# The source and the piece size of ten accumulating DMAs in a weight-streaming decoder layer

## The chip, the cores and the metric

The kernel runs on one core of a Trainium2 chip. The metric is the device time of one execution in microseconds; lower is better. The time of a version is the median of its runs.

## The reference, cut to what matters

One layer of a decoder trunk is computed for 256 tokens of width 2048, all in float32: a gated conformer branch and a block-sparse attention branch, cross attention to 256 memory tokens, and a SwiGLU feed-forward part. The change touches only the feed-forward part, whose first product takes most of its weights' bytes:

```
def swiglu(h, w_in, w_out):
    g, u = jnp.split(h @ w_in, 2, axis=-1)
    return (jax.nn.silu(g) * u) @ w_out
...
        h = rmsnorm(x, norm_ffn_g[l])
        x = x + swiglu(h, w_ffn_in[l], w_ffn_out[l])
```

`w_ffn_in` has 2048 rows and 2 x 5632 columns.

## The kernel before, in words

**Split products.** Each float32 matrix product is made of three passes of TensorE. Both factors are split into a high part (the value rounded to float32r, a narrower format that TensorE takes at full rate) and a low part (the value minus its high part). `mm3` (lines 426 to 431) then issues high x high (L429), high x low of the weights (L430) and low x high (L431). L430 is thus the first line that reads the weights' low part.

**Blocks, pairs, units.** The weights are streamed from DRAM once. A block covers 1024 columns of a weight matrix, two halves of 512, for all rows. The feed-forward part's first product is made of the blocks ffn0 to ffn10, each with 512 columns of the gate half and 512 of the other half, so that a row's two pieces lie far apart in DRAM. A block walks over 8 pairs of 128 rows (1 MB of weights each, 4 pieces of 512 columns on 128 partitions). A pair is either one plain unit (kind W, 8 products of `mm3`) or two units of a scheme of Strassen's kind with 7 products (kinds a and b), for which VectorE first forms sums of the four pieces.

**Places.** A pair's weights land in a raw place (`raw`, 1 MB); during the feed-forward blocks there are five. They are loaded by SP in the order of the pairs, four DMAs of 256 KB a pair (`load_unit`, lines 719 to 736), each as soon as the place is free; SP's queue works in order, so that a load that waits holds all loads behind it. The high and the low part of a unit stand in a place for weights, one of five in this part, called `whi`/`wlo` or `w` in the profile. TensorE's last product with it makes it free.

**The usual way.** ScalarE casts `raw` to the high part (`cast_one`), VectorE subtracts it from `raw` and writes the low part (`step_one`, L832, shown as L97 in the profile, the line of a wrapper round all such calls). Then the raw place is free.

**The way of ten units.** `ADDED_LOW` (line 39) names pair 0 of each of ffn1 to ffn10. For these, `subtract_on_way` (lines 738 to 744) lets ScalarE write the negated high part into the low part's place. Then GpSimd issues DMAs that add the raw weights to it as they are written (`accum_op`). VectorE has no part in it. Before the change, these DMAs read the weights a second time from DRAM: two DMAs, one for each half of 512 columns, each of 128 partitions x 2 rows x 2 KB. The raw place is free after ScalarE's cast.

**What sets the order.** The order of all engines' instructions is written out when the program is built, by a planner that keeps an estimated clock of TensorE, VectorE, ScalarE and the loads (`self.clock`). `ADDED = 8.0` (line 40) is its estimate of the microseconds from ScalarE's end to the low part's landing; `leave_raw` (lines 844 to 848) tells it when a raw place is free. The semaphore waits follow from which instruction reads and writes which place. Beside these ten units GpSimd moves other things by DMA: in the feed-forward part it writes the block's results to DRAM (L1997, `md`) and reads them back later (L2026).

## Time and profile before

| | |
|---|---|
| median of 3 runs | 1709.81 us (1707.27 to 1713.94) |
| the profiled execution's own time | 1708.28 us |
| its span, first to last instruction | 1706.5 us |
| granted TensorE clock | 0.997 |
| ScalarE (ACT) busy | 1035.5 us, 61% of the span |
| read from DRAM | 351.97 MB |

The engines are PE (TensorE's products), PEld (its weight loads), DVE (VectorE), ACT (ScalarE), POOL (GpSimd) and SP (SyncE, which issues loads). A name with q stands for the engine's sequencer. Tiles are named out<-in without buffer numbers, so `w<-in_w_ffn_in` is a transfer from the weights in DRAM to a place for weights. Rows of waits give who waited for what, the sum in us, how often and the longest. Rows of the timeline give the start and the duration in us, the instruction, and in brackets the idle time just before it and what ended it; x8 there stands for several of one form in a row. Rows of the chain give start, duration and what the chain ran through.

### The profile page before, as it was taken

The numbers are of one execution on the slowest core, as the hardware profiler recorded it, in microseconds if no ns is written. First come the engines' busy times: TensorE is split into PE (matmuls) and PEld (weight loads), VectorE is DVE, ScalarE is ACT, GpSimd is POOL, SyncE is SP. The second block draws the span as 40 slices with busy tenths as digits, with TensorE's granted clock in tenths as the row PEclk, the third lists the DMA queues.
The fourth block names the chain that finished last, engine by engine and source line by source line (L and its number), as shares of the span: only waits on it lengthen the run. The fifth ranks groups of instructions, "written<-read, shape, count | busy, mean of one in ns | idle before, by whom it ended". The sixth has DMA issues, their size and how long they took to land. (4 is left out here: it accounts for less than half of the span.)

```text
span 1706.5 us, 20882 instructions
## 1 busy us (share of the span) xinstructions
PE 1668.4 (98%) x7586; PEld 1377.8 (81%) x7586; DVE 1448.9 (85%) x1470; ACT 1035.5 (61%) x1142; POOL 88.7 (5%) x147
## 2 busy tenths in 40 slices
PE   9999999999999999999999999999999999999998
PEld 7888888888888888888888877787777777888886
DVE  7889989898778898977888989878878877999797
ACT  7565768887545686655556665555555545665563
POOL 0000000000000010000001000000000001110100
PEclk9999999999999999999999999999999999999999
DMA  8656555566666776645556778677667767787773
GB/s 290 215 205 219 192 186 179 172 217 205 196 209 208 228 241 209 210 148 186 174 173 203 277 221 252 197 211 239 208 208 230 211 205 234 241 295 246 263 236 124
DMA packets 147479, 365.42 MB, mean 214 GB/s; under 512 B 17040, under 2 KB 17296, under 8 KB 147376
## 3 DMA queue, kind: packets, MB, share of 16 engines
q1 hardware_dynamic: 131904, 322.36, 57.5%
q0 software_dynamic: 14608, 40.54, 8.3%
q8 instruction: 59, 0.97, 0.2%
q10 hardware_dynamic: 864, 1.19, 0.2%
q14 instruction: 44, 0.36, 0.1%
HBM read 351.97 MB, written 12.06 MB: 213 GB/s over the span
## 5 line engine op out<-in xcount | busy, mean ns | idle before, releaser
L97 DVE TENSOR_TENSOR wlo<-raw,whi 128x1024 fp32r<-128x1024 f32 (+3 forms) x234 | 397.5, 1707 | 77.8 <-ACT whi L97 75.6
L97 ACT CAST whi<-raw 128x1024 fp32r<-128x1024 f32 (+3 forms) x237 | 341.6, 1448 | 135.2 <-PE bank L431 109.0
L430 PE MATMUL bank<-wlo,op 128*128 128x512 f32 x911 | 356.6, 391 | 8.7 <-DMA wlo<-in_w_ffn_in 8.7
L429 PE MATMUL bank<-whi,op 128*128 128x512 f32 x911 | 358.9, 394 | 0.0
L431 PE MATMUL bank<-whi,op 128*128 128x512 f32 x911 | 356.1, 391 | 0.0
L430 PE MATMUL bank<-w,op 128*128 128x512 f32 x750 | 293.7, 392 | 17.8 <-DMA w<-in_w_ffn_in 17.6
L429 PE MATMUL bank<-w,op 128*128 128x512 f32 x750 | 294.7, 393 | 0.0
L431 PE MATMUL bank<-w,op 128*128 128x512 f32 x750 | 292.2, 390 | 0.0
L97 DVE TENSOR_TENSOR w<-raw,w 128x1536 fp32r<-128x1536 f32 (+2 forms) x100 | 203.8, 2041 | 20.7 <-ACT w L97 19.8
L97 ACT CAST w<-raw 128x2048 fp32r<-128x2048 f32 (+2 forms) x107 | 184.1, 1727 | 45.1 <-PE bank L431 26.4
L430 PEld LDWEIGHTS bank<-wlo,op 128*128 128x128 f32 x911 | 171.8, 189 | 46.1 <-DMA wlo<-in_w_ffn_in 11.5
L431 PEld LDWEIGHTS bank<-whi,op 128*128 128x128 f32 x911 | 171.6, 188 | 36.1
L429 PEld LDWEIGHTS bank<-whi,op 128*128 128x128 f32 x911 | 171.8, 189 | 34.4
L430 PEld LDWEIGHTS bank<-w,op 128*128 128x128 f32 x750 | 140.8, 188 | 51.2 <-DMA w<-in_w_ffn_in 22.3
L429 PE MATMUL bank<-whi,xh 128*128 128x512 f32 x449 | 178.4, 397 | 0.2 <-ACT whi L97 0.2
L430 PE MATMUL bank<-wlo,xh 128*128 128x512 f32 x449 | 175.3, 390 | 0.3
L431 PE MATMUL bank<-whi,xl 128*128 128x512 f32 x449 | 175.1, 390 | 0.0
L431 PEld LDWEIGHTS bank<-w,op 128*128 128x128 f32 x750 | 140.8, 188 | 29.2
L429 PEld LDWEIGHTS bank<-w,op 128*128 128x128 f32 x750 | 140.8, 188 | 28.1
L97 ACT CAST w<-sums 128x2048 fp32r<-128x2048 f32 x42 | 80.4, 1914 | 84.1 <-DVE sums L97 59.7
L97 DVE TENSOR_TENSOR w<-sums,w 128x2048 fp32r<-128x2048 f32 x42 | 96.1, 2289 | 25.1 <-ACT w L97 24.9
L97 DVE TENSOR_TENSOR c<-bank,c 128x512 f32<-128x512 f32 x153 | 102.5, 686 | 5.3 <-PE bank L431 0.4
(218 smaller groups left out, 2111.8 us busy)
## 6 DMA issues: line engine op xcount, KB each, us to landing
raw<-in_w_ffn_in SPq DMA_DIRECT2D x352, 256.0 KB, 4.3
raw<-in_w_in SPq DMA_DIRECT2D x84, 512.0 KB, 4.2
raw<-in_w_ffn_out SPq DMA_DIRECT2D x62, 512.0 KB, 5.1
raw<-in_w_ckv SPq DMA_DIRECT2D x48, 512.0 KB, 4.5
raw<-in_w_in SPq DMA_DIRECT2D x72, 256.0 KB, 4.5
raw<-in_w_ffn_out SPq DMA_DIRECT2D x52, 256.0 KB, 4.7
raw<-in_w_out SPq DMA_DIRECT2D x24, 512.0 KB, 5.1
raw<-in_w_cq SPq DMA_DIRECT2D x24, 512.0 KB, 5.1
```

The source lines that it names most:

```text
L97: return f(out, *args, **kwargs)
L429: mm(out, lhs[0], rhs[0], start=start, stop=False)
L430: mm(out, lhs[0], rhs[1], start=False, stop=False)
L431: mm(out, lhs[1], rhs[0], start=False, stop=stop)
```

## The change

The accumulating DMAs of the ten units read the raw weights from their raw place in SBUF and no longer from DRAM. The two DMAs become one, over the whole 128 x 2048 tile, so that each partition's piece is one run of 8 KB in source and destination. The raw place is now read by this DMA, so that SP's next load into it waits for its landing too; the planner is told that it is free `ADDED` later.

```
-    def subtract_on_way(self, x, hi, lo):
+    def subtract_on_way(self, src, hi, lo):
 
         self.act.activation(lo, hi.bitcast(F32), AF.Copy, scale=-1.0)
-        rows = slice(2 * x.p * P, (2 * x.p + 2) * P)
-        for j, (w, c) in enumerate(x.blk.cols):
-            self.nc.gpsimd.dma_start(
-                lo[:, j::2, :], w[rows, c : c + 512].rearrange("(i p) n -> p i n", p=P), accum_op=ALU.add)
+        lo, src = (y.rearrange("p a n -> p (a n)") for y in (lo, src))
+        self.nc.gpsimd.dma_start(lo, src, accum_op=ALU.add)
...
         if x.added:
-            self.subtract_on_way(x, *self.w[v])
-            self.leave_raw(x, t["act"])
+            self.subtract_on_way(src, *self.w[v])
+            self.leave_raw(x, t["act"] + ADDED)
```

In the built program the order of the instructions of every engine is the same before and after, apart from the ten DMAs that stand in place of twenty on GpSimd. Ten loads of SP, one in each of ffn1 to ffn10, wait for one more semaphore.

## The prediction

> **What bounds the kernel now.** I read the page's shares first, then the waits of TensorE, then the chain of work round one of those waits.

> ```profile
> PE 1668.4 (98%) x7586; PEld 1377.8 (81%) x7586; DVE 1448.9 (85%) x1470; ACT 1035.5 (61%) x1142; POOL 88.7 (5%) x147
> PE 28%; DMA 7%; ACT 1%; issue 1%; DVE 1%; POOL 0%; DVEq 0%; ACTq 0%
> ```

> TensorE is busy for 98% of 1706.5 us, so it idles for 1706.5 - 1668.4 = 38.1 us in all, and an edit can only win from that idle time (and from the restarts after it). The second row is the chain that ended last: 7% of it is DMA, far more than ScalarE or VectorE. The list of TensorE's waits says which DMA:

> ```profile
> PE bank L430 <- DMA w<-in_w_ffn_in: 17.6, 13, 2.3
> PE bank L430 <- DMA wlo<-in_w_ffn_in: 8.7, 6, 2.3
> ```

> Only the accumulating DMAs of L743 write `w` or `wlo` from `in_w_ffn_in` (plain loads write `raw`). So 17.6 + 8.7 = 26.3 us of the 38.1 us, in 13 + 6 = 19 waits, are TensorE standing at line 430, the first product that reads a low part, until such a DMA lands. There are ten such units, the first pair of each of the blocks ffn1 to ffn10, two DMAs each; 19 of the 20 are late, by 26.3 / 10 = 2.63 us a block. The chain through ffn3 shows how:

> ```profile
> 1088.20 0.24 PE bank L431
> ...
> 1088.51 1.93 ACT w L97
> ...
> 1090.46 1.93 ACT w L97
> ...
> 1092.68 0.43 POOL w L743
> ...
> 1093.38 13.84 DMA w<-in_w_ffn_in
> ...
> 1107.27 0.50 PE bank L430
> ```

> TensorE frees a place for weights at 1088.4, ScalarE casts the high part and writes the negated copy (2 x 1.93 us), GpSimd issues at 1092.68, and the second DMA (issued at 1093.38) lands 13.84 us later. The start of this chain hangs on TensorE's own earlier work, so the room from GpSimd's issue to TensorE's need stays as it is when everything shifts.

> **What a wait costs beyond its idle time.** Four products in a row, the third after a stop without recorded idle time:

> ```profile
> 1005.66 0.39 PE L431 MATMUL bank<-w,op 128*128 128x512 f32 x1
> 1005.89 0.39 PE L429 MATMUL bank<-w,op 128*128 128x512 f32 x1
> 1006.29 0.50 PE L430 MATMUL bank<-w,op 128*128 128x512 f32 x1
> 1006.62 0.40 PE L431 MATMUL bank<-w,op 128*128 128x512 f32 x1
> ```

> Starts are 0.23 us apart while TensorE runs; here they are 0.40 and 0.33. So a stop loses (0.40 - 0.23) + (0.33 - 0.23) = 0.27 us on top of recorded idle time (a product's recorded time overlaps the next one's). For 19 waits: 5.1 us. If all the waits go, the gain is 26.3 + 5.1 = **31.4 us**.

> **When the low part is needed.** Issue and need, in three blocks (ffn3, ffn8, ffn9; ffn3's issue stands above):

> ```profile
> 1103.38 0.50 PE L430 MATMUL bank<-w,op 128*128 128x512 f32 x1 [1.81 <-DMA w<-in_w_ffn_in]
> 1107.27 0.50 PE L430 MATMUL bank<-w,op 128*128 128x512 f32 x1 [1.79 <-DMA w<-in_w_ffn_in]
> ```
> ```profile
> 1321.07 2.45 POOL L743 DMA_DIRECT2D wlo<-in_w_ffn_in  x2 [22.75 <-DVE sums L97]
> 1366.26 2.39 POOL L743 DMA_DIRECT2D w<-in_w_ffn_in  x2 [42.74 <-DVE sums L97]
> ```
> ```profile
> 1330.64 0.50 PE L430 MATMUL bank<-wlo,op 128*128 128x512 f32 x1 [0.67 <-DMA wlo<-in_w_ffn_in]
> 1376.25 0.50 PE L430 MATMUL bank<-w,op 128*128 128x512 f32 x1 [1.89 <-DMA w<-in_w_ffn_in]
> ```

> The first need is the start less the idle time: 1101.57, 1329.97 and 1374.36, which is 8.89, 8.90 and 8.10 us after the issue. Before, the first columns' DMA meets that need and the second columns' DMA may come 2 products later. After, one DMA serves both, so all of its 1 MB has to land within about 8.1 to 8.9 us; before, the second landing came at 13.8 us in ffn3 (the answer for line 743 in that window):

> ```profile
> DMA to landing us min/median/max: 10.7/12.3/13.8
> ```

> **When the new DMA lands.** No trace here shows an accumulating DMA from SBUF or one with 8 KB pieces, so I bound it. Rows of the DMA view for 1000 to 1426 us, and of the landing times of line 1997 (256 KB, SBUF to DRAM, plain):

> ```profile
> q1 hardware_dynamic: 43285, 78.83, 57.5%
> q0 software_dynamic: 6800, 14.94, 16.2%
> ...
> md<-mid POOLq DMA_DIRECT2D x18, 256.0 KB, 4.1
> ```
> ```profile
> DMA to landing us min/median/max: 2.3/4.0/6.5
> ```

> The window holds 426 x 16 = 6816 us of DMA engines. Plain loads: 57.5% = 3919 us for 78.83 MB, 49.7 us a MB. GpSimd's queue: 16.2% = 1104 us; less 18 x 0.262 = 4.72 MB of `md` at 49.7 (235 us) leaves 869 us for 10.2 MB of accumulation, 85 us a MB. So 1.05 MB of accumulation costs 1.05 x 85 / 16 = 5.6 us of all engines, and at the plain price it would cost 3.3 us. Fixed part: the fastest `md` takes 2.3 us, of which 0.26 x 49.7 / 16 = 0.8 is data, so 1.5 us. That gives 1.5 + 3.3 = 4.8 us as the low end. The high end is the old pair's 13.8 us. I take 1.5 + 5.6 = **7.1 us**, the accumulating rows' own price per byte, since nothing shows that a longer piece or the other source changes it.

> The old 13.8 us is long because the engines were full of loads at the same time (share and GB/s at the end of the row):

> ```profile
> 1101.50:1107.50 6.00, 2.40 (x12) 1.75 (x12) 6.00 (x8) 1.89 (x3) 0.59 (x1) 1.00 0.99 265
> ```

> The edit removes that rivalry by a side effect: the raw place is no longer free at the cast but when the accumulating DMA has landed, and SP's queue is in order. SP's next load into that place waits, and all loads behind it stand too:

> ```profile
> 1090.45 0.33 SPq L735 DMA_DIRECT2D raw<-in_w_ffn_in  x1
> ...
> 1092.30 5.60 SPq L731 DMA_DIRECT2D raw<-in_w_ffn_in  x8
> 1109.57 0.33 SPq L735 DMA_DIRECT2D raw<-in_w_ffn_in  x1
> ```

> In ffn3 the load at 1090.45 is the one that waits; these 4 + 8 loads, 3 MB, mostly ran beside the accumulation before and come behind it after. So the DMA runs nearly alone there: 7.1 us against 8.9 of room, no wait. In ffn1, ffn2, ffn5 and ffn8 one whole load (4 issues, 1 MB, 3.3 us of all engines) goes out just ahead of the one that waits, as here in ffn8:

> ```profile
> 1319.13 0.33 SPq L735 DMA_DIRECT2D raw<-in_w_ffn_in  x1
> ```

> It is about half done when the accumulation starts, so I add 1.5 us: 8.6 us against 8.9. Too close to call; I allow 0.35 us of wait and a restart in three of these blocks (ffn1 had no first wait, so it has more room): 3 x 0.62 = 1.9 us.

> [...]

> **What the held loads cost.** In ffn3 SP's load slips from 1090.45 to 1092.68 + 7.1 = 1099.8, 9.3 us. The 3 MB then need 3 x 3.3 = 9.9 us, so the first MB is there at about 1099.8 + 5 = 1105 and the last at about 1111. ScalarE first reads the first of them here:

> ```profile
> 1114.01 3.53 ACT L97 CAST w<-raw 128x2048 fp32r<-128x2048 f32 x2
> ```

> If this is 3.6 us earlier after, 1110.4, some 5 us remain. ffn1 has the least room:

> ```profile
> 1002.12 0.38 SPq L735 DMA_DIRECT2D raw<-in_w_ffn_in  x1
> ```
> ```profile
> 1023.11 1.91 ACT L97 CAST w<-raw 128x2048 fp32r<-128x2048 f32 x1
> ```

> Issue at 1001.34 + 8.6 = 1010 and 5 us to land make 1015 against 1023. I cost the hold at nothing; its cover is the loads' lead over the casts, and without the cover each late us would count once a block, 10 us in all.

> **What is late next.** VectorE and ScalarE could keep TensorE's old pace. But what they idle for after a block's start is TensorE itself:

> ```profile
> 1245.09 0.59 ACT L97 COPY mid<-bank 128x512 f32<-128x512 f32 x1 [6.74 <-PE bank L443]
> ```
> ```profile
> 1246.33 0.75 DVE L97 SCALAR_TENSOR_TENSOR raw<-c,ss,raw 128x512 f32<-128x512 f32 x1 [3.53 <-ACT raw L97]
> ```

> ScalarE waited 6.74 us for transposes that stand behind the late products, VectorE 3.53 us behind ScalarE. Both move with TensorE, so no new wait. GpSimd issues one DMA in place of two (10 fewer), and nothing on it was late. DRAM reads fall by 10.5 MB, of no worth by itself. The engines' instructions and their order are otherwise the same.

> **The sum.** 31.4 - 1.9 = 29.5 us. The profiled execution took 1708.28 us, so 1678.8; it lies 1.5 us under the median of the three runs (1709.81), so the median after is 1680.3, say **1680**.

> **The rivals.** (a) The accumulation is dearer or is cut into the old 2 KB pieces (the change would then not do what it says): with 4 x 128 pieces the issue would take about as long as now, 2.4 us in place of some 0.6, so 7.1 + 1.8 = 8.9, or 10 us beside loads. At 9.9 us each block waits 1.2 + 0.27, 14.7 us in all: 1709.8 - 31.4 + 14.7 = **1693**. For it: nothing shows 8 KB pieces. Against it: even so it beats 13.8. (b) Slower: one landing for both halves. TensorE's first products no longer go ahead with half of the low part; if the DMA lands at x us, a block loses x - 8.7 + 0.27 where it lost 2.63 + 0.51 = 3.14, so it decides from x = 11.6. At twice the price, 1.5 + 11.2 = 12.7 us, it loses 4.3: 10 x 1.13 = 11 us slower, **1721**; at the old 13.8, 22 us slower, 1732. For it: both operands and the result now lie in SBUF, in the same partitions. Against it: the engines are emptied of loads. (c) The held loads come late to the casts by 2 to 3 us a block and eat the gain: 1680 + 25 = **1705**. Against it: the 5 and 8 us left above.

> **Chances and range.** Forecast (1674 to 1686) 0.70; (a) 1686 to 1700, 0.13; (c) and other near-draws 0.07; (b) 0.10. The range runs from 1674 (all waits gone, and 4 us as the runs before scatter) to 1697, which leaves out (b), (c) and a part of (a), some 0.2. Faster by over 0.5% (8.5 us, about what a measurement of this kernel can tell from no change): 0.83; within 0.5%: 0.07; slower: 0.10.

> **What would show it.** In the profile after: ten accumulating DMAs of 1 MB that land 7 to 9 us after their issue; TensorE's waits for them under 3 us in total where 26.3 stood; SP's wait for these DMAs, about 7 to 9 us in each block; a DMA share that falls to the accumulation alone while it runs; no new wait of ScalarE for `raw`. Landings over 11.6 us, or casts that wait for `raw`, would prove me wrong.

## The result, and the profile after

The changed kernel took **1681.36 us** (median of 4 runs, 1679.54 to 1682.95) against 1710.66 us for the kernel before (4 runs, 1707.27 to 1713.94): a ratio of 0.9829 (95% interval 0.9806 to 0.9851). Its profiled execution took 1681.37 us with a span of 1679.6 us, 26.9 us under the span before. The accumulating DMA is L742 there, the load issues keep L731 to L736, and the lines behind the change stand two lower.

The page's shares and its chain of the kernel after:

```profile
PE 1663.9 (99%) x7586; PEld 1378.5 (82%) x7586; DVE 1448.1 (86%) x1470; ACT 1033.4 (62%) x1142; POOL 72.6 (4%) x137
...
PE 89%; DMA 5%; DVE 3%; issue 1%; ACT 1%; SPq 0%; DVEq 0%; ACTq 0%; POOLq 0%
```

TensorE now idles for 1679.6 - 1663.9 = 15.7 us where it idled for 38.1; that is 22.4 of the 26.9 us. The other 4.5 us are less busy time for the same 7586 products. TensorE's waits after (sum, times, longest):

```profile
PE bank L430 <- DVE wlo L97: 1.5, 1, 1.5
PE bank L430 <- DMA wlo<-raw: 1.3, 1, 1.3
PE bank L430 <- DMA w<-raw: 1.0, 1, 1.0
```

The 19 waits on the accumulating DMAs (26.3 us) have become two (2.3 us), and there is one new wait of 1.5 us on VectorE. The answer for the accumulating line, and the DMA share while one of its ten DMAs runs (ffn3's, us, PE, PEld, DVE, ACT, POOL, granted clock, DMA share, GB/s):

```profile
L742 POOL DMA_DIRECT2D w<-raw x7: 863/886/891, 1003.5 to 1388.1; - x7
L742 POOL DMA_DIRECT2D wlo<-raw x3: 874/886/891, 1050.4 to 1303.3; - x3
...
DMA to landing us min/median/max: 7.0/7.8/9.3
```
```profile
1093.50:1098.70 5.20, 5.20 (x25) 4.30 (x24) 2.26 (x3) 3.75 (x3) 0.00 (x0) 1.00 0.93 187
```

Ten DMAs land 7.0 to 9.3 us after their issue, where the second of a pair landed up to 13.9 us after its own issue. While ffn3's runs, nothing else does: 187 GB/s over 5.2 us is 0.97 MB, nearly the DMA's own 1.05 MB, against 265 GB/s of mixed traffic before. SP shows why. Its queue stands until the landing (the waits of SP on these DMAs, and the issues of ffn3, which stood at 1090.45 before):

```profile
SPq L735 <- DMA w<-raw: 79.3, 7, 13.0
...
SPq L731 <- DMA wlo<-raw: 27.2, 3, 9.2
```
```profile
1099.00 0.33 SPq L735 DMA_DIRECT2D raw<-in_w_ffn_in  x1
...
1100.85 4.23 SPq L731 DMA_DIRECT2D raw<-in_w_ffn_in  x8
```

The change moves three things at once: the source (DRAM or SBUF), the number and piece size of the DMAs (two of 2 KB or one of 8 KB), and the hold of SP's loads until the landing. The theory to test was the prediction's: the **hold** wins, because the DMA then runs alone. The rivals: the **source**, and the **pieces**.

### The profile page after: what moved, and what is told of

It is laid out like the page before. It is cut to its first block, busy times and chain, and to the rows that moved or that the text cites. A ratio compares the mean times of both kernels' runs of the same rounds, so it can differ in the third digit from the quotient of the medians.

```text
span 1679.6 us, 20886 instructions
## 1 busy us (share of the span) xinstructions
PE 1663.9 (99%) x7586; PEld 1378.5 (82%) x7586; DVE 1448.1 (86%) x1470; ACT 1033.4 (62%) x1142; POOL 72.6 (4%) x137
## 4 chain that ended last, share of the span: by engine, by line
PE 89%; DMA 5%; DVE 3%; issue 1%; ACT 1%; SPq 0%; DVEq 0%; ACTq 0%; POOLq 0%
PE bank L430 29%; PE bank L431 29%; PE bank L429 29%; PE bank L443 2%; DMA raw<-in_w_ffn_in 2%; DMA wlo<-raw 2%; DMA w<-raw 1%; DVE w L97 1%; DVE sums L97 1%; DVE wlo L97 1%; ACT w L97 0%; DVE c L97 0%; ACT whi L97 0%; DMA vecs<-in_vecs 0%; PE bank L1547 0%
## 5 line engine op out<-in xcount | busy, mean ns | idle before, releaser
L97 DVE TENSOR_TENSOR wlo<-raw,whi 128x1024 fp32r<-128x1024 f32 (+3 forms) x234 | 397.6, 1707 | 76.7 <-ACT whi L97 74.9
L97 ACT CAST whi<-raw 128x1024 fp32r<-128x1024 f32 (+3 forms) x237 | 341.3, 1447 | 131.0 <-PE bank L431 106.5
L430 PE MATMUL bank<-wlo,op 128*128 128x512 f32 x911 | 355.3, 390 | 3.0 <-DVE wlo L97 1.5
L429 PE MATMUL bank<-whi,op 128*128 128x512 f32 x911 | 357.8, 393 | 0.0
L431 PE MATMUL bank<-whi,op 128*128 128x512 f32 x911 | 354.9, 390 | 0.0
L429 PE MATMUL bank<-w,op 128*128 128x512 f32 x750 | 294.6, 393 | 0.0
L430 PE MATMUL bank<-w,op 128*128 128x512 f32 x750 | 292.3, 390 | 1.2 <-DMA w<-raw 1.0
L431 PE MATMUL bank<-w,op 128*128 128x512 f32 x750 | 292.2, 390 | 0.0
L97 DVE TENSOR_TENSOR w<-raw,w 128x1536 fp32r<-128x1536 f32 (+2 forms) x100 | 203.9, 2041 | 17.8 <-ACT w L97 17.8
L97 ACT CAST w<-raw 128x2048 fp32r<-128x2048 f32 (+2 forms) x107 | 183.9, 1726 | 45.2 <-PE bank L431 28.8
L430 PEld LDWEIGHTS bank<-wlo,op 128*128 128x128 f32 x911 | 171.2, 188 | 39.0 <-DMA wlo<-raw 2.7
L431 PEld LDWEIGHTS bank<-whi,op 128*128 128x128 f32 x911 | 171.0, 188 | 35.9
L429 PEld LDWEIGHTS bank<-whi,op 128*128 128x128 f32 x911 | 171.1, 188 | 34.3
L429 PE MATMUL bank<-whi,xh 128*128 128x512 f32 x449 | 179.5, 400 | 0.2 <-ACT whi L97 0.2
L430 PE MATMUL bank<-wlo,xh 128*128 128x512 f32 x449 | 176.2, 392 | 0.1
L431 PE MATMUL bank<-whi,xl 128*128 128x512 f32 x449 | 176.0, 392 | 0.0
L430 PEld LDWEIGHTS bank<-w,op 128*128 128x128 f32 x750 | 140.9, 188 | 30.4 <-DMA w<-raw 1.3
L431 PEld LDWEIGHTS bank<-w,op 128*128 128x128 f32 x750 | 140.8, 188 | 29.5
L429 PEld LDWEIGHTS bank<-w,op 128*128 128x128 f32 x750 | 140.9, 188 | 28.1
L97 ACT CAST w<-sums 128x2048 fp32r<-128x2048 f32 x42 | 80.4, 1914 | 92.2 <-DVE sums L97 81.5
L97 DVE TENSOR_TENSOR w<-sums,w 128x2048 fp32r<-128x2048 f32 x42 | 96.2, 2290 | 17.2 <-ACT w L97 17.1
L97 DVE TENSOR_TENSOR c<-bank,c 128x512 f32<-128x512 f32 x153 | 102.6, 687 | 5.3 <-PE bank L431 0.4
## 6 DMA issues: line engine op xcount, KB each, us to landing
raw<-in_w_ffn_in SPq DMA_DIRECT2D x352, 256.0 KB, 4.6
raw<-in_w_in SPq DMA_DIRECT2D x72, 256.0 KB, 4.6
raw<-in_w_ffn_out SPq DMA_DIRECT2D x52, 256.0 KB, 4.5
```

Of the source, the lines that this page charges most:

```text
L97: return f(out, *args, **kwargs)
L429: mm(out, lhs[0], rhs[0], start=start, stop=False)
L430: mm(out, lhs[0], rhs[1], start=False, stop=False)
L431: mm(out, lhs[1], rhs[0], start=False, stop=stop)
```

## The experiments

Medians, with the ratio to the runs of the kernel before on the same chip:

| kernel | source | DMAs | loads held | us (range) | ratio (95%) |
|---|---|---|---|---|---|
| after | SBUF | 1, 8 KB | yes | 1681.36 (1679.54 to 1682.95) | 0.9829 (0.9806 to 0.9851) |
| two_sbuf | SBUF | 2, 2 KB | yes | 1674.69 (1674.54 to 1675.35) | 0.9795 (0.9781 to 0.9810) |
| two_sbuf_swapped | SBUF | 2, 2 KB, late one first needed | yes | 1680.27 (1678.72 to 1681.30) | 0.9820 (0.9804 to 0.9836) |
| dram_hold | DRAM, a rest from SBUF | 2, 2 KB, and a small one | yes | 1676.61 (1674.45 to 1677.29) | 0.9803 (0.9787 to 0.9820) |
| longer_hold | SBUF | 1, 8 KB | longer | 1683.28 (1682.08 to 1686.75) | 0.9845 (0.9825 to 0.9865) |
| no_hold | SBUF | 1, 8 KB | no | 1716.64 (1715.59 to 1721.05) | 1.0044 (1.0027 to 1.0060) |
| two_no_hold | SBUF | 2, 2 KB | no | 1713.98 (1710.64 to 1718.34) | 1.0016 (1.0004 to 1.0028) |
| swapped_dram | DRAM | 2, 2 KB, late one first needed | no | 1741.78 (1738.59 to 1746.40) | 1.0189 (1.0168 to 1.0210) |
| swapped_warm | the same | the same, with extra products | no | 1727.50 (1726.38 to 1731.82) | 1.0101 (1.0082 to 1.0121) |

**two_sbuf: the new source and the hold, with the two DMAs of before.** Against the kernel after:

```
-        lo, src = (y.rearrange("p a n -> p (a n)") for y in (lo, src))
-        self.nc.gpsimd.dma_start(lo, src, accum_op=ALU.add)
+        for j in range(2):
+            self.nc.gpsimd.dma_start(lo[:, j::2, :], src[:, j::2, :], accum_op=ALU.add)
```

> Two DMAs of 512 KB from the raw place in SBUF, one for each half of the columns, with 2 KB pieces: the source and the hold of the changed kernel, the number and the piece size of the kernel before. Theory H (the held loads leave the DMA engines to the accumulation, and that is what makes it land early; source and piece size count little): the first DMA lands 5 to 6 us after its issue, the second 7.5 to 9 us after the first issue, TensorE waits under 4 us in total for them, time 1678 to 1685 us. Rival P (the long pieces or the single DMA make it fast): the second lands 10 to 13 us after the issue as before the change, waits of 10 to 25 us, 1693 to 1706 us.

1674.69 us, below the expected range and faster than the kernel after (every run of the one lies below every run of the other, though the intervals of the two ratios overlap). TensorE's only wait on the DMAs, and the landings of its twenty DMAs:

```profile
PE bank L430 <- DMA wlo<-raw: 0.8, 1, 0.8
```
```profile
DMA to landing us min/median/max: 5.1/7.4/9.6
```

The first halves land as early as 5.1 us after their issue. One landing for both halves therefore costs something: the change's own step to one DMA takes back 4 to 6 us of what the rest gains. (Between the two profiled executions it is 6.0 us, but 2.0 of them are a slow start of the kernel after that the edit does not touch; it is shown below.)

**two_sbuf_swapped: the same pair in the other order**, so that the first products need the later DMA, as they need the only DMA of the kernel after. Against two_sbuf:

```
-        for j in range(2):
+        for j in (1, 0):
```

> The two DMAs from SBUF with 2 KB pieces and the hold, issued in the other order, so that TensorE's first products need the one that lands last (it landed 7.6 to 10.4 us after the first issue in the run with the right order). Theory E (two DMAs beat one because the half that is needed first lands at 5 to 6 us): it gives that back and is no better than the single DMA: 1679 to 1685 us, waits of 2 to 6 us in total in the blocks where loads run beside. Rival: the 2 KB pieces themselves, or what runs beside them, are better: 1673 to 1677 us as with the right order.

1680.27 us, 5.6 us back (4.3 us by the ratios, as the two ran on different chips) and 1.1 us from the kernel after. TensorE's waits:

```profile
PE bank L430 <- DMA w<-raw: 2.3, 4, 1.4
PE bank L430 <- DMA wlo<-raw: 2.0, 3, 1.5
```

The waits and their restarts, 3.5 + 6 x 0.27 = 5.1 us, make up the 5.2 us between the two spans (1678.8 and 1673.6). So it is the early landing of the first half that two_sbuf has over the kernel after, and the piece size leaves no difference in the time that I could tell from these runs' scatter.

**dram_hold: the old source, with the hold.** The two DMAs read DRAM as before; the last 64 columns of the second half are added by a small third DMA from the raw place, which holds SP's loads:

```
+        for j, (w, c) in enumerate(x.blk.cols):
+            n = 512 - 64 * j
+            self.nc.gpsimd.dma_start(
+                lo[:, j::2, 0:n], w[rows, c : c + n].rearrange("(i p) n -> p i n", p=P), accum_op=ALU.add)
+        self.nc.gpsimd.dma_start(lo[:, 1::2, n:], src[:, 1::2, n:], accum_op=ALU.add)
```

> Two DMAs from DRAM with 2 KB pieces as before, but the last 64 columns of the second half come from the raw place by a third, small DMA, so that the raw place is held until about the landing and SP's loads wait (all but one 256 KB load in most blocks). Theory H: the accumulation runs nearly alone though its source is DRAM: second landing 8 to 9.5 us after the first issue, the small one within 1 us more, waits of 2 to 10 us in total, time 1681 to 1692 us. Rival P (SBUF source or long pieces needed): landings of 10 to 13 us, 1698 to 1712 us.

1676.61 us, below the expected range. TensorE's waits on the DMAs, and SP's:

```profile
PE bank L430 <- DMA wlo<-raw: 1.4, 2, 1.0
```
```profile
SPq L736 <- DMA w<-raw: 72.6, 7, 10.6
...
SPq L731 <- DMA wlo<-raw: 29.9, 3, 10.2
```

More than the whole gain of the change is there, 33.9 us, with 15 of 16 weights still read from DRAM. The source is not the cause.

**no_hold: the new source and the one DMA, without the hold.** The DMA adds another tile of SBUF of the same shape (a left factor), so that the raw place is free at the cast as before; the ten units' low parts are other numbers:

```
-        lo, src = (y.rearrange("p a n -> p (a n)") for y in (lo, src))
-        self.nc.gpsimd.dma_start(lo, src, accum_op=ALU.add)
+        lo = lo.rearrange("p a n -> p (a n)")
+        self.nc.gpsimd.dma_start(lo, self.lefts["x3"]["quad"][0].bitcast(F32), accum_op=ALU.add)
...
-            self.leave_raw(x, t["act"] + ADDED)
+            self.leave_raw(x, t["act"])
```

> One DMA with 8 KB pieces from SBUF as in the changed kernel, but it adds another tile (a constant left factor of the feed-forward part) and not the raw weights, so the low parts hold other numbers, and SP's loads are not held. Theory H: 1.1 to 1.5 MB of loads run beside it, the first packet comes late, it lands 9.5 to 11.5 us after the issue, TensorE waits 1 to 2.5 us in each block, time 1692 to 1706 us. Rival P (the long pieces take the engines by themselves): it lands within 9 us, time 1679 to 1686 us.

1716.64 us, 0.4% slower than before and dearer than I expected. TensorE's waits, and the landings:

```profile
PE bank L430 <- DMA w<-op: 19.4, 6, 4.3
PE bank L430 <- DMA wlo<-op: 8.6, 3, 3.5
```
```profile
DMA to landing us min/median/max: 10.0/11.9/12.6
```

Without the hold the one DMA lands at a median of 11.9 us in place of 7.8, and TensorE waits 28.0 us in 9 long waits where the kernel before had 26.3 us in 19. The whole gain, and a little more, is gone with the hold. The waits alone are 1.7 us longer than before; most of the 12.8 us between the two spans (1719.3 and 1706.5) goes with the granted clock, 0.989 against 0.997, and 0.008 x 1719 is 14 us.

**two_no_hold: the new source with the two DMAs of before, without the hold.** The same stand-in tile in no_hold's loop of two:

```
+        src = self.lefts["x3"]["quad"][0].bitcast(F32).rearrange("p (a n) -> p a n", a=4)
+        for j in range(2):
+            self.nc.gpsimd.dma_start(lo[:, j::2, :], src[:, j::2, :], accum_op=ALU.add)
```

> Two DMAs from SBUF with 2 KB pieces that add a constant left factor and not the raw weights (the low parts hold other numbers), so that SP's loads are not held: against the kernel before only the source differs. Theory H: the source counts little, the loads beside it set the landing: first 9 to 10.7 us, second 11.5 to 14 us, waits of 22 to 30 us, 1704 to 1714 us. Rival S (reading SBUF and not DRAM speeds the accumulation): second landing under 10.5 us, 1680 to 1695 us.

1713.98 us (10 runs). Waits and landings are those of before (26.3 us in 19; 9.0/11.1/13.9):

```profile
PE bank L430 <- DMA w<-op: 15.4, 12, 2.3
PE bank L430 <- DMA wlo<-op: 11.1, 6, 2.3
```
```profile
DMA to landing us min/median/max: 9.3/11.1/13.8
```

This kernel differs from the one before in the source alone (with other numbers in it), and its DMAs land no sooner for it.

**longer_hold: the hold made longer.** Behind each accumulating DMA of the kernel after, a plain DMA copies the raw place to a scratch place in DRAM, which keeps it occupied some microseconds more:

```
+        self.nc.gpsimd.dma_start(self.marks["scratch"], src)
```

> The changed kernel, and behind each accumulating DMA a plain DMA of the same 1 MB from the raw place to a scratch tensor in DRAM, which nothing reads: the loads are held some 3 to 4 us longer and the engines move 10.5 MB more. Theory H says the loads' lead over the casts covers a hold of 7 to 9 us with 1 to 9 us to spare (the least in ffn7 and ffn4), so a longer hold begins to show there: ScalarE waits for loads of up to 3 us in two to four blocks, TensorE behind it for less, 1681 to 1690 us. Rival (the lead is far larger than needed): no change, 1679 to 1683 us. Rival (the loads were already the limit): 10 x 3 us more, 1705 us or over.

1683.28 us, 2 us over the kernel after. SP's waits on these DMAs:

```profile
SPq L735 <- DMA scratch<-raw: 63.4, 7, 15.3
SPq L731 <- DMA scratch<-raw: 35.9, 3, 12.4
...
SPq L735 <- DMA w<-raw: 35.1, 3, 12.0
```

SP stood for 134.4 us in place of 106.5, and it cost about 2 us, which is within the scatter of the two kernels. ScalarE waits long for weights of the feed-forward's first product only once, 7.4 us in ffn1, and for a load that goes out ahead of the hold. The loads' lead over the casts covers the hold with room left.

**swapped_dram: what a later first landing costs.** The kernel before with its two DMAs issued in the other order, so that the first products need the later one:

```
-        for j, (w, c) in enumerate(x.blk.cols):
+        for j, (w, c) in reversed(list(enumerate(x.blk.cols))):
```

> The kernel before, with its two DMAs from DRAM issued in the other order, so that TensorE's first products need the DMA that lands last: the same as one landing for both halves, at the landing time of before. By the break-even of the prediction (a block loses x - 8.9 + 0.27 us where it lost 3.14, with second landings of 12.3 to 14.6 us, 13.3 on average) it is 10 x 1.5 = 15 us slower than before: 1720 to 1732 us, ten waits of 3.5 to 6 us each. Rival: which half comes first does not matter, because TensorE meets the second landing in either case: 1707 to 1714 us.

1741.78 us, more than I expected. TensorE's waits, its busy time, and two stretches round ffn2's wait of 4.83 us (which ends at 1063.99), with the granted clock third from the end:

```profile
PE bank L430 <- DMA w<-in_w_ffn_in: 29.7, 7, 5.7
PE bank L430 <- DMA wlo<-in_w_ffn_in: 14.9, 3, 5.1
```
```profile
PE 1682.8 (97%) x7586; PEld 1391.4 (80%) x7586; DVE 1449.1 (83%) x1470; ACT 1035.0 (60%) x1142; POOL 88.4 (5%) x147
```
```profile
1062.00:1064.00 2.00, 0.01 (x1) 0.01 (x1) 2.00 (x2) 0.17 (x1) 0.00 (x0) 0.86 1.06 327
1064.00:1066.00 2.00, 2.00 (x5) 1.61 (x6) 2.00 (x3) 0.00 (x0) 0.00 (x0) 0.50 0.66 208
```

The waits are 44.6 - 26.3 = 18.3 us longer, which the landings explain. The other 14.4 us are busy time, 1682.8 against 1668.4 for the same products: after the wait TensorE's granted clock is 0.50, and products start 0.43 us apart instead of 0.23. (The 0.23 us are those of a float32r product of 512 columns at the clock 1.00; a plain float32 one of 256 columns takes 0.43 us at 1.00, as at 300.20 us in the kernel after, L1599.) Some 2 us of the 14.4 lie ahead of the ten blocks (the first accumulating DMA is issued at 1003.5 us and in the kernel before at 1001.3), and ten waits in place of 19 save about as much in restarts.

**swapped_warm: the same, with TensorE kept busy.** Ahead of each of the ten late units, 14 products of 128x512 into a bank that nothing reads fill a part of the wait:

```
+        for _ in range(14):
+            self.nc.tensor.matmul(self.banks[i], lh[:, 0:P], w[0][:, 0, :], start=True, stop=True)
```

> The kernel before with its DMAs in the other order, and 14 extra products (128x512, 3.2 us in all, into a bank that nobody reads) ahead of each of the ten late units, so that TensorE is busy in most of the wait. Theory C (the wait costs more than its idle time because the granted clock falls to half for one or two windows of 3.4 us after it): the drops go, and with them up to 14 us of slower products: 1726 to 1732 us, granted clock 0.995 or more. Rival (the price is the late landing alone, or the extra work adds to it): 1740 us or more.

1727.50 us: **more** products, and 14.3 us less, for landings as late as in swapped_dram (9.5/10.9/14.1 us against 9.1/10.9/13.3). The granted clock rises from 0.985 to 0.997. TensorE's busy time, and what is left of the waits:

```profile
PE 1698.5 (98%) x7726; PEld 1405.1 (81%) x7726; DVE 1448.8 (84%) x1470; ACT 1035.0 (60%) x1142; POOL 88.4 (5%) x147
```

```profile
PE bank L430 <- DMA w<-in_w_ffn_in: 8.9, 5, 2.8
PE bank L430 <- DMA wlo<-in_w_ffn_in: 5.5, 3, 2.3
```

The 140 extra products fill waiting time, 140 x 0.23 = 32 us; the 7586 others are left with some 1666 us, where they took 1682.8 in swapped_dram (1.8 us of this lie ahead of the ten blocks). So a part of what a long wait costs is the slow clock behind it, and that part can be had back without a shorter wait.

## Why the prediction was right, point by point

**What bounds the kernel and what goes.** Right. The 26.3 us of waits fell to 2.3 us on these DMAs, or 3.8 us with the new wait on VectorE: 22.5 us. With 19 waits down to 3, restarts at the prediction's 0.27 us give 4.3 us. The two make 26.8 us of the 29.5 that were forecast from waits and restarts.

**The landing, 7.1 us.** Right where nothing else ran: ffn3, 4, 6, 7 and 9 land 6.96 to 7.13 us after the issue. The price of 85 us a MB was a little high; by the stretch of ffn3 above, 0.93 x 5.2 x 16 / 0.97 MB is 80. The one DMA of long pieces is the cheaper way here: the two of 2 KB pieces have landed 7.6 to 10.4 us after the first issue in two_sbuf.

**The four blocks with a load just ahead, 8.6 us.** Right in kind, but too small: ffn1, 2, 5 and 8 land at 8.91 to 9.31 us. Only ffn2 waits long for it, 1.28 us. ffn10 was to be quiet and still landed at 8.57 us and waited 1.03 us. Nothing of SP's was under way then; the DMA view from 1391 to 1396 us shows one fetch of instructions (packets, MB, share of 16 engines), 0.012 x 16 x 5 = 0.96 us of one engine:

```profile
q0 software_dynamic: 96, 0.66, 65.8%
q8 instruction: 1, 0.02, 1.2%
```

Three last pieces start one by one until 1395.67, 0.61 us apart, which I read as the work of a single engine, when all others have started by 1394.1; the landing at 1396.64 follows the last. No run moves a fetch, so that it is the cause is argued only.

**The need, 8.1 to 8.9 us after the issue.** Somewhat generous: the prediction held that this room stays as it was before, and in two blocks it shrank by 0.8 us. ffn2's products were ready at 1059.79 - 1.28 = 1058.51, 8.1 us after the issue at 1050.43 (before 8.9), and ffn10's at 1395.65, 7.6 us after 1388.07 (before 8.35). That is one reason why two_sbuf, whose first half lands earlier, is faster.

**The held loads cost nothing.** Right for the ten held loads; longer_hold shows that some 3 us more a block costs 2 us in all. The new wait on VectorE came by another way: ffn1's load just **ahead** of the hold, issued from 1002.42 on. It ran beside the accumulation before the change too, but beside one DMA of 8 KB pieces it is later: its last 256 KB took 8.9 us to land, against 5.8 before. The source has no part in that: this wait of 1.5 us stands in the three kernels with one DMA (after, no_hold, longer_hold) and in none with two, whether they read SBUF (two_sbuf, two_no_hold) or DRAM (before). The cast that needs the load, before and then after:

```profile
1007.45 1.49 ACT L97 CAST w<-raw 128x1536 fp32r<-128x1536 f32 x1 [2.33 <-DMA raw<-in_w_ffn_in]
```
```profile
1012.70 1.48 ACT L97 CAST w<-raw 128x1536 fp32r<-128x1536 f32 x1 [5.42 <-PE bank L431]
...
1021.67 0.50 PE L430 MATMUL bank<-wlo,op 128*128 128x512 f32 x1 [1.54 <-DVE wlo L97]
```

After names TensorE as the cast's releaser, but the load's last part landed at 1012.61, which is what the cast at 1012.70 follows. no_hold has the same delay with the load named:

```profile
1011.05 1.48 ACT L97 CAST w<-raw 128x1536 fp32r<-128x1536 f32 x1 [5.91 <-DMA raw<-in_w_ffn_in]
```

**What is late next: nothing.** Right but for this one wait of 1.5 us. By the prediction's own sign, no new wait of ScalarE for `raw`, this cast is a miss.

**A term that the sum lacked: the clock.** The prediction held that an edit can only win from idle time and restarts. But two of the old waits were followed by the slow clock in the profile of before: stretches from 1061.1 and 1194.2 us (third from the end the granted clock), and the first product of each after its wait:

```profile
1061.10:1064.50 3.40, 3.40 (x10) 2.66 (x9) 3.33 (x5) 0.00 (x0) 0.00 (x0) 0.50 0.72 227
1194.20:1197.60 3.40, 2.83 (x6) 1.72 (x6) 3.40 (x4) 0.72 (x1) 0.00 (x0) 0.50 1.07 313
```
```profile
1060.20 0.50 PE L430 MATMUL bank<-wlo,op 128*128 128x512 f32 x1 [2.31 <-DMA wlo<-in_w_ffn_in]
...
1194.13 0.76 PE L430 MATMUL bank<-wlo,op 128*128 128x512 f32 x1 [1.88 <-DMA wlo<-in_w_ffn_in]
```

Each costs half of TensorE's busy time in it, 1.7 and 1.4 us, and both are gone after: 3.1 us. The profiled start of the kernel after took most of that away; in the first 14 us TensorE does 45 products before and 35 after (two_sbuf: 44), and after begins ffn0 2.15 us later:

```profile
0.00:14.00 14.00, 11.02 (x45) 8.85 (x46) 7.20 (x12) 9.72 (x16) 2.35 (x13) 1.00 0.89 311
```
```profile
0.00:14.00 14.00, 11.17 (x35) 8.98 (x36) 7.05 (x12) 8.88 (x15) 2.34 (x13) 1.00 0.87 306
```

The edit touches nothing there. I take it to be the clock again, though this column says 1.00 (the trace's first record of the clock begins at 6.37 us before and at 12.13 us after): products start 0.23 us apart before and 0.43 us apart after, as they do at 0.50 in swapped_dram, and from 12.17 us on 0.23 us apart after too. Two starts of each:

```profile
8.47 0.40 PE L429 MATMUL bank<-whi,xh 128*128 128x512 f32 x1
8.70 0.40 PE L430 MATMUL bank<-wlo,xh 128*128 128x512 f32 x1
```
```profile
7.93 0.63 PE L429 MATMUL bank<-whi,xh 128*128 128x512 f32 x1
8.36 0.63 PE L430 MATMUL bank<-wlo,xh 128*128 128x512 f32 x1
```

Together 22.5 + 4.3 + 3.1 - 2.15 = 27.8 us against 26.9 measured between the two spans; 0.9 us stay unexplained. That the forecast of 29.5 us lies so near the 29.3 between the medians is partly luck: the waits and restarts brought 2.7 us less than forecast, and the drops of the clock, which were not in the sum, seem to have made up for it. The scatter of the kernel before goes largely with this clock: of its runs with the clock on record, the four at 0.997 took 1707.7 to 1709.6 us, the six at 0.992 to 0.994 took 1710.1 to 1714.3.

**The rivals.** (a) fell: two_sbuf, with four 2 KB pieces for each 8 KB one, is faster, not slower, as one landing and not the piece size is what costs. (b), one landing for both halves, has a true mechanism (two_sbuf against two_sbuf_swapped, 4 to 6 us) but its landings of 7 to 9.3 us stayed below the break-even of 11.6. Its price beyond that was too low: where the prediction had only idle time and 0.27 us, swapped_dram lost 14.4 us more in busy time, 1.4 us a block. no_hold shows the point in place: landings of 11.9 us, at (b)'s break-even, and a time 0.4% over before. (c) was wrong: the hold costs next to nothing.

**The source and the pieces.** The stretch of ffn3 takes 5.2 us, a little under the prediction's 5.6 us, and the source makes no difference: with the hold, two_sbuf's DMAs from SBUF and dram_hold's from DRAM both land at a median of 7.4 us, so that the ground given for (b), both operands and the result in SBUF, shows in no landing. Beside loads the whole MB lands sooner as one DMA, at a median of 11.9 us and at most 12.6 (no_hold), where the landings of the two go up to 13.8 us after their own issue (two_no_hold); the load in ffn1 lands later for it, 8.9 us against 5.8 as above. Why the long pieces get on faster there was not shown. For TensorE it was worth nothing, because the first columns' share came later (no landing under 10.0 us in no_hold, the earliest at 9.3 us in two_no_hold).

## What to carry to other kernels

When a transfer on the critical path is late, look first at what shares the DMA engines with it: here holding back early loads for 9 to 13 us a block, which had time to spare, was worth 34 to 39 us in three pairs of kernels (after and no_hold, two_sbuf and two_no_hold, dram_hold and before), and neither the source nor the piece size was worth anything that could be measured in the time. Keep a late transfer in parts that land in the order of their use; merging two DMAs into one cost 4 to 6 us. Here the version to take is two_sbuf, 0.9795 of before, which keeps the hold and the two DMAs.

## What was not expected of the hardware

```profile
1057.67:1061.08 3.41, 1.09 (x5) 0.75 (x5) 3.41 (x4) 0.72 (x1) 0.00 (x0) 1.00 0.99 304
1190.79:1194.20 3.41, 1.53 (x8) 0.95 (x6) 3.27 (x6) 2.00 (x2) 0.00 (x0) 1.00 1.10 260
...
1330.74:1334.15 3.41, 1.57 (x6) 0.95 (x6) 3.41 (x5) 0.72 (x1) 0.00 (x0) 1.00 1.09 289
```

Over these two profiles, 4 of 982 steps at the full clock were followed by a drop (two of them at the kernels' ends), and TensorE was busy for at most 1.53 us of each; in the other 978 steps it was busy for at least 1.57 us. So a wait of 1.9 us was enough where it lay in one step, and 1.57 us of busy time in a step were enough against a drop. This is read from the traces; no run moves a wait along the grid. In swapped_dram, with waits up to 5.7 us, such drops cost some 14 us, and 14 unread products ahead of each late unit brought the granted clock from 0.985 back to 0.997: by an estimate from these, some 10 us at half clock (2 x 0.003 x 1724.6) in place of 52 (2 x 0.015 x 1739.1).
